# Down projection in four blocks instead of three, with its operands fetched piece by piece ahead of time

## The chip, the cores and the metric

The kernel runs on one NeuronCore of a Trainium2 chip. Its engines are TensorE (PE, with its weight loads shown apart as PEld), VectorE (DVE), ScalarE (ACT), GpSimd (POOL) and SyncE (SP), which here only issues DMAs. The metric is device time in microseconds (us) for one execution, the median of several.

## The reference

One layer of a decoder for 1024 prompt tokens with 16 meta tokens ahead of them, and for 8 running sequences of 4 tokens each. A short convolution and a multi-head retention mix the tokens, `w_out` projects the result back, and a SwiGLU network follows. Only this last part matters here:

```
xn = _rmsnorm(x, norm2_g)
x  = x + (silu(xn @ w_gate) * (xn @ w_up)) @ w_down      # 1024 -> 2816 -> 1024
y  = _rmsnorm(x, final_norm_g)
```

## The kernel before

All activations stand transposed: features on the 128 partitions, the 1056 tokens along the free dimension, cut into two halves `g` of 528 columns (`HT`). Every fp32 operand is split into a high and a low part; a product is three matmuls (high by high, high by low, low by high).

**Gate and up.** The hidden width of 2816 is 22 tiles of 128 (`f`). For each `f` the function `strassen` computes gate and up together by a Winograd scheme with seven products instead of eight. Their right-hand operands (`comb`) are 7 combinations of 8 tiles each; these 56 tiles stand in the pool `rows`, which has 62 buffers of one shape. The results of two neighbouring `f` make a "pair"; `spill` and `spill_plain` write 7 combinations of a pair, or the plain tiles of the last four `f`, to DRAM (`hd`, `hp`), high and low parts apart, 264 KB each, through POOL's queue (`to_hd`, whose two parts take `rows` buffers too).

**Down.** `w_down` is applied in `DBLOCKS`, three blocks of 3 pairs each, and then in a plain part for the last four `f`. A block fetches its 42 operand tiles (7 keys x 3 pairs x 2 parts) from `hd` into `rows` buffers with `pull` (L886 to L889), all ahead of its first matmul in the program's order. Then four iterations over two rows of output tiles (`m`) follow. Each loads four pieces of `w_down` (`load_w`, five buffers `wraw`) and runs `strassen`.

In `strassen`, `product` splits one weight (ACT writes `whi` at L153, DVE writes `wlo` at L155, four buffers each) and then issues its matmuls (L762): pairs x 2 token sets x 3, so 18 for three pairs. Four of the weights are sums that `total` makes on DVE (L750), in buffers `s` of the current pool. The order is `y1 z1 y2 w1 y3 z2 y4` over three accumulators in PSUM (`dy`, `dz`, `dw` in the rows). After each product `on` adds the accumulator to a running sum `x1[m][g]` in SBUF (L913, 128 x 528). So `y2` can write `dy` only when the addition after `y1` has read it.

The 16 tiles `x1` start from the residual, which lies in DRAM as `x1d`. They are allocated in the pool `fin`, which is opened where the pool `late` (gate and up results, the sums of that part) is closed; `fin` takes over its memory. Their loads (L907) stand behind the loads of `w_down` in each iteration of the first block.

The framework orders the instructions of each engine and queue itself when the program is built: an instruction can be placed once its buffer is available, and among those the program's order decides. SP issues its DMAs one after the other, so one that waits for a buffer holds up all behind it.

Of the kernel before, what the change touches and what calls it, by code (L numbers as in the profile page):

```python
# [10 lines left out]
F32 = mybir.dt.float32  # L11
F32R = mybir.dt.float32r
# [4 lines left out]
P = 128  # L17
# [14 lines left out]
KT = DM // P  # L32
NFF = 22
# [12 lines left out]
HT = 528  # L46
# [1 line left out]
PO = [240, 512]  # L48
NDP = 9
NPL = NFF - 2 * NDP  # L50
DBLOCKS = [(0, 3), (3, 6), (6, 9)]

C_CONV_B, C_CONV_C, C_CONV_H, C_Q, C_K, C_V, C_G = 0, 4, 8, 12, 16, 20, 24

# [58 lines left out]
def _build(nc, t, offs, ncols):  # L113
    with tile.TileContext(nc) as tc:
        _body(nc, tc, t, offs, ncols)


def _body(nc, tc, t, offs, ncols):
    PSUM = bass.MemoryType.PSUM
    V, S, G, T, D = nc.vector, nc.scalar, nc.gpsimd, nc.tensor, nc.sync  # L120
    HW = SW // 2
    with contextlib.ExitStack() as ctx:
# [7 lines left out]
        def ut(name, dt=F32):  # L130
            return rows.tile([P, SW], dt, tag="u", name=name)
# [14 lines left out]
        def load_w(ap, n):  # L146
            raw = wts.tile([P, 512], F32, tag="wraw", name="wraw", bufs=5)
            D.dma_start(raw[:, :n], ap)
            return raw
# [48 lines left out]
        def rms_compact(sets, name):  # L198
            blocks = [(i, o, min(P, w - o)) for i, (_, w) in enumerate(sets) for o in range(0, w, P)]
            tot = len(blocks)  # L200
            ps = aux.tile([P, 512], F32, tag="aux", name=name + "p")
            a = cst.tile([P, 16], F32, tag="rms", name=name + "a", bufs=6)
            V.memset(a, 1.0)
            for q in range(len(sets[0][0])):
                for i, (c, o, n) in enumerate(blocks):
                    T.matmul(ps[:n, q * tot + i:q * tot + i + 1], sets[c][0][q][:, o:o + n], ones[:, 0:1],
                             start=True, stop=True)
                i = 0
                while i < tot:
                    j, n = i, blocks[i][2]  # L210
                    while j < tot and blocks[j][2] == n:
                        j += 1
                    if q == 0:
                        V.tensor_scalar(a[:n, i:j], ps[:n, i:j], 1.0 / DM, EPS, ALU.mult, ALU.add)
                    else:
                        V.scalar_tensor_tensor(a[:n, i:j], ps[:n, q * tot + i:q * tot + j], 1.0 / DM, a[:n, i:j],
                                               ALU.mult, ALU.add)
                    i = j
            r = cst.tile([P, 16], F32, tag="rms", name=name + "r", bufs=6)
            tmp = cst.tile([P, 16], F32, tag="rms", name=name + "t", bufs=6)  # L220
            rsqrt(r[:, :tot], a[:, :tot], tmp[:, :tot])
            return r, blocks
# [17 lines left out]
        with contextlib.ExitStack() as mid_ctx:  # L240
# [46 lines left out]
            for k in range(KT):  # L287
# [5 lines left out]
                for s in range(SETS):  # L293
                    if k == 0 and s == 0:
                        h = SW // 2
# [21 lines left out]
            for k in range(KT):  # L317
                for s in range(SETS):
                    n = WALL[s]
# [25 lines left out]
            for s in range(SETS):  # L345
                n = WALL[s]
# [309 lines left out]
        def gg(name):  # L656
            return late.tile([P, SW], F32, tag="gg", name=name, bufs=9)

        def tt(name):
            return late.tile([P, HW], F32, tag="tt", name=name, bufs=4)  # L660
# [5 lines left out]
        for f in range(4):  # L666
            w = w_in(C_G + f)
            for s in range(SETS):
                n = WTOK[s]
                ps = proj(w, xn[s], ntok[s], "pg")  # L670
                x = gg("gt")
# [5 lines left out]
        x1d = dram.tile([KT, 2, P, HT], F32, name="x1d")  # L677
        hd = dram.tile([NDP, 7, 2, P, HT], F32, name="hd")
        hp = dram.tile([NPL, 2, 2, P, HT], F32, name="hp")
# [12 lines left out]
        def norm2(s):  # L692
            n = ntok[s]
            st = [([sums2[s]], WTOK[s])]
            r, bl = rms_compact(st, f"n2{s}")
            yield
            rms_rows(r, bl, st, f"n2{s}",
                     [[(rstd2[g][:, SO[s]:SO[s] + n], g * n, n) for g in range(2)]])
            yield

        for s in range(SETS):
            n = ntok[s]
            ss2 = late.tile([P, SW], F32, tag="rr", name="ss2", bufs=2)
            half = None
            for m in range(KT):
                x = gg("x1")
# [11 lines left out]
                if m % 2 == 0:  # L718
                    c = {"b11": build(s, xg[:, :n], "b11")}
                    t1 = tt("t1")  # L720
# [3 lines left out]
                else:  # L724
                    c["b21"] = build(s, xg[:, :n], "b21")
                    t2, t3, t4 = tt("t2"), tt("t3"), tt("t4")
# [97 lines left out]
        def up_rhs(s, k, key, part):  # L824
            return comb[s][k][key][:, part, :ntok[s]]

        pending = iter(())
        n2g = norm2(1)
        held = None
        for f in range(NFF):  # L830
            wg, wu = t["w_gate"][f], t["w_up"][f]
            a11 = load_w(wg[:, :512], 512)
            a21 = load_w(wu[:, :512], 512)
            a22 = load_w(wu[:, 512:], 512)
            a12 = load_w(wg[:, 512:], 512)
            gt = [gg("gt") for _ in range(2)]
            up = [gg("up") for _ in range(2)]

            def on(step, ps):
                if step == "y1":  # L840
                    S.activation(gt[0][:, :HT], ps, AF.Copy)
                elif step == "z1":
                    S.activation(up[1][:, :HT], ps, AF.Copy)
                elif step == "y2":
                    S.activation(up[0][:, :HT], ps, AF.Copy)
                elif step == "w1":
                    V.tensor_tensor(gt[0][:, :HT], ps, gt[0][:, :HT], ALU.add)
                elif step == "y3":
                    V.tensor_tensor(up[1][:, :HT], ps, up[1][:, :HT], ALU.add)  # L849
                elif step == "z2":  # L850
                    V.tensor_tensor(up[0][:, :HT], ps, up[0][:, :HT], ALU.add)
                else:
                    V.tensor_tensor(gt[1][:, :HT], ps, rstd2[1], ALU.mult)
                if step == "w1":
                    V.tensor_tensor(gt[0][:, :HT], gt[0][:, :HT], rstd2[0], ALU.mult)
                if f == 0 and step in ("y1", "z1"):
                    next(n2g)
                next(pending, None)

            strassen(late, a11, a21, a22, a12, 512, 4, up_rhs, "b", on)  # L860
            for g in range(2):
                x, y = gt[g][:, :HT], up[g][:, :HT]
                S.activation(x, x, AF.Silu)
                V.tensor_tensor(y, y, rstd2[g], ALU.mult)
                V.scalar_tensor_tensor(y, y, -1.0, x, ALU.mult, ALU.mult)
            for _ in pending:
                pass
            if f >= 2 * NDP:
                pending = spill_plain(f - 2 * NDP, *up)
            elif f % 2 == 0:  # L870
                held = up
            else:
                pending = spill(f // 2, *held, *up)
# [4 lines left out]
        fin = ctx.enter_context(tc.tile_pool(name="fin", bufs=1))  # L878
# [1 line left out]
        def tf(name):  # L880
            return fin.tile([P, HW], F32, tag="tt", name=name, bufs=5)

        KEYS = ("b11", "t3", "t2", "b21", "t1", "t4", "b22")
        x1 = [[fin.tile([P, HT], F32, name=f"x1_{m}_{g}") for g in range(2)] for m in range(KT)]

        def pull(src, name):  # L886
            x = ut(name, F32R)
            D.dma_start(x.bitcast(F32)[:, :HT], src)
            return x  # L889

        for bi, (p0, p1) in enumerate(DBLOCKS):
            nk = p1 - p0
            hs = {key: [[pull(hd[p, i, part], "h" + key) for part in range(2)] for p in range(p0, p1)]
                  for i, key in enumerate(KEYS)}

            def dn_rhs(s, k, key, part):
                return hs[key][k][part][:, SO[s]:SO[s] + ntok[s]]

            for m in range(0, KT, 2):
                w = nk * P  # L900
                at = 2 * p0 * P
                a11, a21 = (load_w(t["w_down"][m + i][:, at:at + w], w) for i in range(2))
                a22, a12 = (load_w(t["w_down"][m + i][:, at + w:at + 2 * w], w) for i in (1, 0))
                if bi == 0:
                    for i in range(2):
                        for g in range(2):
                            D.dma_start(x1[m + i][g], x1d[m + i, g])  # L907

                def on(step, ps):
                    i, g = {"y1": (0, 0), "z1": (1, 1), "y2": (1, 0), "w1": (0, 0), "y3": (1, 1), "z2": (1, 0),  # L910
                            "y4": (0, 1)}[step]
                    x = x1[m + i][g]
                    V.tensor_tensor(x, x, ps, ALU.subtract if i else ALU.add)  # L913

                strassen(fin, a11, a21, a22, a12, w, nk, dn_rhs, "d", on)

        hs = [[[pull(hp[i, g, part], "hp") for part in range(2)] for g in range(2)] for i in range(NPL)]
        wd = []
        for m in range(KT):
            raw = load_w(t["w_down"][m][:, 2 * NDP * P:], 512)  # L920
# [20 lines left out]
        for s in range(SETS):  # L941
            for g in range(2):
                n = ntok[s]
                ss3 = tf("ss3")
                for m in range(KT):
# [9 lines left out]
                    x = x1[m][g][:, SO[s]:SO[s] + n]  # L955
# [14 lines left out]
def _host(inp):  # L970
# [13 lines left out]
    for name in ("w_gate", "w_up"):  # L984
        w = f[name][0].reshape(KT, P, NFF * P)[order].reshape(DM, NFF * P)
        a[name] = tiles(w, NFF)
    order = [2 * p + i for p0, p1 in DBLOCKS for i in range(2) for p in range(p0, p1)] + list(range(2 * NDP, NFF))
    a["w_down"] = tiles(f["w_down"][0].reshape(NFF, P, DM)[order].reshape(NFF * P, DM), KT)
# [41 lines left out]
```

## Time and profile before

| what | value |
|---|---|
| median of 3 runs | 1240.03 us (1238.91 to 1240.71) |
| the profiled execution | 1237.07 us |
| its span from the first to the last instruction | 1235.2 us |
[...]
| TensorE busy | 1197.7 us, 97% |
| VectorE busy | 824.0 us, 67% |

The span is what the trace covers; the profiled execution's time is 1.9 us longer. Times in the rows below count from the span's start. The last gate and up step (`f` = 21) runs until 961.8 us, the down blocks from there to 1167.9 us, the plain part and the final norm to the end.

### The profile page before, as it was taken

What the parts mean: (1) busy time and instruction counts of PE and PEld (TensorE: products, weight loads), DVE (VectorE), ACT (ScalarE), POOL (GpSimd) and SP (SyncE); (2) the same over time, 40 slices, a digit from 0 to 9 for tenths busy, and PEclk for the clock granted to TensorE, in tenths of its full rate; (3) what the DMA queues carried; (4) which work ended last, traced back from release to release, by engine and by line L of the source; (5) the groups of instructions that cost most, each with busy time, mean ns of one, the idle gap of its engine ahead of it and who ended that gap; (6) DMA issues with size and microseconds to landing.
All of it is one profiled execution on the core that took longest, in us unless ns stands there. A gap on an engine that the chain in (4) does not pass through costs nothing.

```text
span 1235.2 us, 24336 instructions
## 1 busy us (share of the span) xinstructions
PE 1197.7 (97%) x9769; PEld 1185.0 (96%) x9769; DVE 824.0 (67%) x1520; ACT 480.8 (39%) x904; POOL 121.8 (10%) x251
## 2 busy tenths in 40 slices
PE   8999999999999999999999999999999499999996
PEld 8999988999999999999999999999999499999996
DVE  5355477676454678777977797778775365757665
ACT  8256521121133456534444444444443122212353
POOL 0100121000000112102220222022210000000000
PEclk9999999999999999999999999999999799999998
DMA  6321211101111456324442544255434997666213
GB/s 235 98 70 44 77 44 44 35 18 40 34 53 44 123 172 197 122 74 170 169 144 94 174 166 142 95 175 174 140 125 144 397 303 270 220 239 196 75 40 102
DMA packets 79760, 163.01 MB, mean 132 GB/s; under 512 B 10445, under 2 KB 21472, under 8 KB 79648
## 3 DMA queue, kind: packets, MB, share of 16 engines
q1 hardware_dynamic: 65264, 114.57, 28.6%
q0 software_dynamic: 14384, 46.89, 10.6%
q8 instruction: 77, 1.26, 0.4%
q14 instruction: 35, 0.29, 0.1%
HBM read 113.15 MB, written 48.26 MB: 131 GB/s over the span
## 4 chain that ended last, share of the span: by engine, by line
PE 86%; issue 5%; DMA 4%; DVE 3%; ACT 1%; POOL 1%; SPq 0%; DVEq 0%; POOLq 0%; ACTq 0%
PE by L762 18%; PE bz L762 9%; PE dy L762 9%; PE po L180 6%; PE bw L762 5%; PE dz L762 4%; PE pk L180 4%; PE pc L180 4%; PE pv L180 4%; PE pq L180 4%; PE pg L180 4%; PE pd L951 3%; PE pb L180 3%; PE ph L180 3%; PE dw L762 2%
## 5 line engine op out<-in xcount | busy, mean ns | idle before, releaser
L153 ACT ACTIVATE whi<-wraw 128x512 fp32r<-128x512 f32 (+1 forms) x186 | 113.3, 609 | 317.5 <-issue 63.4
L155 DVE TENSOR_TENSOR wlo<-wraw,whi 128x512 fp32r<-128x512 f32 (+1 forms) x186 | 122.4, 659 | 60.2 <-ACT whi L153 60.1
L153 ACT ACTIVATE whi<-s 128x512 fp32r<-128x512 f32 (+1 forms) x136 | 80.4, 592 | 155.2 <-PE by L762 47.5
L762 PE MATMUL by<-t,whi 128*128 128x256 f32 (+1 forms) x704 | 131.9, 287 | 0.0
L762 PE MATMUL bz<-t,whi 128*128 128x256 f32 (+1 forms) x704 | 131.7, 286 | 0.0
L762 PE MATMUL by<-b,whi 128*128 128x256 f32 (+1 forms) x704 | 129.8, 284 | 0.2 <-DVE up L849 0.2
L155 DVE TENSOR_TENSOR wlo<-s,whi 128x512 fp32r<-128x512 f32 (+1 forms) x136 | 86.9, 639 | 42.6 <-ACT whi L153 42.0
L762 PEld LDWEIGHTS by<-t,whi 128*128 128x128 f32 x704 | 110.3, 190 | 0.0
L762 PEld LDWEIGHTS bz<-t,whi 128*128 128x128 f32 x704 | 109.8, 189 | 0.0
L762 PEld LDWEIGHTS by<-b,whi 128*128 128x128 f32 x704 | 109.3, 188 | 0.4 <-DVE up L849 0.4
L762 PE MATMUL by<-t,wlo 128*128 128x256 f32 (+1 forms) x352 | 100.8, 286 | 0.0
L762 PE MATMUL bz<-t,wlo 128*128 128x256 f32 (+1 forms) x352 | 100.5, 285 | 0.0
L762 PE MATMUL by<-b,wlo 128*128 128x256 f32 (+1 forms) x352 | 100.2, 285 | 0.0
L913 DVE TENSOR_TENSOR x<-x,dy 128x528 f32<-128x528 f32 x48 | 33.8, 704 | 56.2 <-PE dy L762 44.8
L762 PE MATMUL dy<-ht,whi 128*128 128x272 f32 (+1 forms) x288 | 55.7, 291 | 13.7 <-DVE x L913 13.1
L762 PEld LDWEIGHTS by<-t,wlo 128*128 128x128 f32 x352 | 67.0, 190 | 0.0
L762 PEld LDWEIGHTS bz<-t,wlo 128*128 128x128 f32 x352 | 66.6, 189 | 0.0
L762 PEld LDWEIGHTS by<-b,wlo 128*128 128x128 f32 x352 | 66.1, 188 | 0.0
L762 PE MATMUL bw<-b,whi 128*128 128x272 f32 (+1 forms) x352 | 65.5, 285 | 0.0
L788 POOL DMA_DIRECT2D hd<-hh x63 | 34.0, 540 | 284.4 <-ACT hh L786 282.7
L762 PEld LDWEIGHTS dy<-ht,whi 128*128 128x128 f32 x288 | 46.0, 194 | 14.3 <-DVE x L913 13.4
L762 PE MATMUL dz<-ht,whi 128*128 128x272 f32 (+1 forms) x288 | 55.3, 290 | 3.4 <-ACT whi L153 3.4
(303 smaller groups left out, 3194.2 us busy)
## 6 DMA issues: line engine op xcount, KB each, us to landing
ht<-hd SPq DMA_DIRECT2D x72, 264.0 KB, 5.3
hd<-hh POOLq DMA_DIRECT2D x63, 264.0 KB, 3.7
hd<-hl POOLq DMA_DIRECT2D x63, 264.0 KB, 3.7
hb<-hd SPq DMA_DIRECT2D x54, 264.0 KB, 5.3
wraw<-w_in SPq DMA_DIRECT2D x54, 256.0 KB, 2.9
wraw<-w_gate SPq DMA_DIRECT2D x44, 256.0 KB, 2.9
wraw<-w_up SPq DMA_DIRECT2D x44, 256.0 KB, 2.8
wraw<-w_down SPq DMA_DIRECT2D x48, 192.0 KB, 3.5
```

What stands on the lines that cost most here:

```text
L153: S.activation(hi[:, :n], raw[:, :n], AF.Copy)
L155: V.tensor_tensor(lo[:, :n], raw[:, :n], hi.bitcast(F32)[:, :n], ALU.subtract)
L180: T.matmul(ps[:, g, :n], wt[:, sl], xk[part][:, g * n:(g + 1) * n], start=(first and i == 0), stop=(last and i == 2))
L762: T.matmul(out, wt[:, sl], rhs(s, k, key, part), start=(first and k == 0 and i == 0), stop=(k == kt - 1 and i == 2), skip_group_check=not ...
L788: G.dma_start(dst[0], hi.bitcast(F32)[:, :HT])
L913: V.tensor_tensor(x, x, ps, ALU.subtract if i else ALU.add)
L951: T.matmul(ps[:, 0, :n], wt[:, sl], hs[k][g][part][:, SO[s]:SO[s] + n], start=(k == 0 and i == 0), stop=(k == NPL - 1 and i == 2))
```

## The change

The 9 pairs are cut into blocks of 2, 2, 2 and 3 pairs. A block's operand fetches become a generator (`pull_block`, `pull_plain`) that is advanced a few tiles at a time from inside other work: 4 tiles after each of the 7 products of the last gate and up step for block 0 (28 tiles), 1 tile after each of the 28 products of a block for the next block of 2 pairs, 2 tiles per product for the block of 3 pairs, and 1 per product for the 16 tiles of the plain part. What is left is fetched where the block begins. The four first running sums `x1[0..1][0..1]` are moved from `fin` to buffers of `rows`, and their loads stand at the start of the last gate and up step; the other twelve stay in `fin` and are allocated where they are loaded.

```diff
-DBLOCKS = [(0, 3), (3, 6), (6, 9)]
+DBLOCKS = [(0, 2), (2, 4), (4, 6), (6, 9)]
...
+        def pull(src, name, dt=F32R):
+            x = ut(name, dt)
+            D.dma_start(x.bitcast(F32)[:, :HT], src)
+            return x
+
+        def pull_block(b):
+            p0, p1 = DBLOCKS[b]
+            hs = parts[b] = {}
+            for i, key in enumerate(KEYS):
+                hs[key] = []
+                for p in range(p0, p1):
+                    hs[key].append([])
+                    for part in range(2):
+                        hs[key][-1].append(pull(hd[p, i, part], "h" + key))
+                        yield
...
+        def advance(gen, n):
+            for _ in range(n):
+                next(gen, None)
...
         for f in range(NFF):
...
+            if f == NFF - 1:
+                for i in range(2):
+                    for g in range(2):
+                        x1[i][g] = pull(x1d[i, g], "x1", F32)[:, :HT]
+                ahead = pull_block(0)
...
                 next(pending, None)
+                advance(ahead, 4)
...
-        x1 = [[fin.tile([P, HT], F32, name=f"x1_{m}_{g}") for g in range(2)] for m in range(KT)]
...
         for bi, (p0, p1) in enumerate(DBLOCKS):
             nk = p1 - p0
-            hs = {key: [[pull(hd[p, i, part], "h" + key) for part in range(2)] for p in range(p0, p1)]
-                  for i, key in enumerate(KEYS)}
+            for _ in ahead:
+                pass
+            hs = parts[bi]
+            if bi + 1 < len(DBLOCKS):
+                ahead = pull_block(bi + 1)
+                step_n = (DBLOCKS[bi + 1][1] - DBLOCKS[bi + 1][0] + 1) // 2
+            else:
+                ahead, step_n = pull_plain(), 1
...
-                if bi == 0:
+                if bi == 0 and m > 0:
                     for i in range(2):
                         for g in range(2):
+                            x1[m + i][g] = fin.tile([P, HT], F32, name=f"x1_{m + i}_{g}")
                             D.dma_start(x1[m + i][g], x1d[m + i, g])
...
                     V.tensor_tensor(x, x, ps, ALU.subtract if i else ALU.add)
+                    advance(ahead, step_n)
```

## Rows read from the trace of the kernel before

**Rows 1.** The page's part 1: busy us, share, instructions by engine.

```profile
PE 1197.7 (97%) x9769; PEld 1185.0 (96%) x9769; DVE 824.0 (67%) x1520; ACT 480.8 (39%) x904; POOL 121.8 (10%) x251
```

**Rows 2.** Windows of 10 us: length, busy time by engine, clock, DMA share, GB/s.

```profile
960.00:970.00 10.00, 6.65 (x45) 6.35 (x44) 6.84 (x12) 3.76 (x7) 2.16 (x4) 0.87 1.04 396
970.00:980.00 10.00, 3.66 (x28) 3.46 (x26) 2.42 (x5) 1.09 (x3) 0.00 (x0) 0.84 1.04 402
980.00:990.00 10.00, 3.19 (x14) 3.19 (x15) 3.05 (x5) 0.00 (x0) 0.00 (x0) 0.50 1.05 389
```

**Rows 3.** Waits of PE from 962 to 987 us: total, times, longest.

```profile
PE dy L762 <- DVE x L913: 13.1, 1, 13.1
PE dz L762 <- ACT whi L153: 3.4, 1, 3.4
```

**Rows 4.** Timeline of PE, 961 to 995 us: start, us, instruction, idle before.

```profile
961.77 0.41 PE L762 MATMUL dy<-hb,whi 128*128 128x272 f32 x2
...
967.47 0.82 PE L762 MATMUL dz<-ht,whi 128*128 128x272 f32 x2 [3.35 <-ACT whi L153]
...
971.32 0.42 PE L762 MATMUL dw<-hb,whi 128*128 128x272 f32 x2
...
986.81 0.82 PE L762 MATMUL dy<-ht,whi 128*128 128x272 f32 x2 [13.15 <-DVE x L913]
```

**Rows 5.** Timeline of SP's queue, 925 to 1000 us.

```profile
928.11 20.85 SPq L148 DMA_DIRECT2D wraw<-w_down  x4
949.05 3.56 SPq L888 DMA_DIRECT2D hb<-hd  x6
...
976.60 3.70 SPq L888 DMA_DIRECT2D hb<-hd  x6
980.66 2.30 SPq L907 DMA_DIRECT2D x<-x1d  x4
...
998.75 0.85 SPq L888 DMA_DIRECT2D hb<-hd  x2
```

**Rows 6.** Timelines of DVE and ACT around the block's start.

```profile
966.22 1.03 DVE L750 TENSOR_TENSOR s<-wraw 128x384 f32<-128x384 f32 x2
...
986.05 0.70 DVE L913 TENSOR_TENSOR x<-x,dy 128x528 f32<-128x528 f32 x1 [11.30 <-DMA x<-x1d]
...
966.89 0.52 ACT L153 ACTIVATE whi<-s 128x384 fp32r<-128x384 f32 x1 [1.45 <-DVE s L750]
```

**Rows 7.** Chain that ended last, down blocks: start, us, work.

```profile
1035.01 2.20 PE dw L762 x18
...
1066.44 2.19 PE dw L762 x18
...
1097.05 2.19 PE dw L762 x18
...
1128.68 2.17 PE dw L762 x18
...
1167.92 15.05 PE pd L951 x120
```

**Rows 8.** Groups by form, 990 to 1168 us: busy, mean ns, idle before.

```profile
L913 DVE TENSOR_TENSOR x<-x,dy 128x528 f32<-128x528 f32 x47 | 33.1, 704 | 44.9 <-PE dy L762 44.8
...
L155 DVE TENSOR_TENSOR wlo<-s,whi 128x384 fp32r<-128x384 f32 x44 | 24.3, 552 | 0.9 <-ACT whi L153 0.7
...
L153 ACT ACTIVATE whi<-s 128x384 fp32r<-128x384 f32 x44 | 23.1, 524 | 68.5 <-PE dy L762 43.4 <-PE dz L762 14.5 <-DVE s L750 9.2
```

**Rows 9.** Groups by form, VectorE, 1168 to 1220 us: an operation 256 wide.

```profile
L956 DVE TENSOR_TENSOR x<-pd,x 128x256 f32<-128x256 f32 x14 | 5.8, 421 | 4.3 <-PE pd L951 4.2
```

**Rows 10.** Timeline of DVE, 880 to 905 us: operations close behind each other.

```profile
882.19 0.71 DVE L799 TENSOR_TENSOR dt<-up 128x528 f32<-128x528 f32 x1
882.81 0.70 DVE L803 TENSOR_TENSOR dt<-up 128x528 f32<-128x528 f32 x1
```

**Rows 11.** Timeline of ACT, 1040 to 1062 us: the first weight of block 1.

```profile
1048.78 0.53 ACT L153 ACTIVATE whi<-wraw 128x384 fp32r<-128x384 f32 x1 [6.71 <-DMA wraw<-w_down]
```

More of the change, by code (lines that the diff above doesn't have):

```diff
@@ L825, in up_rhs, with pull_plain @@
             return comb[s][k][key][:, part, :ntok[s]]
+        KEYS = ("b11", "t3", "t2", "b21", "t1", "t4", "b22")
+        def pull(src, name, dt=F32R):
+            x = ut(name, dt)
+            D.dma_start(x.bitcast(F32)[:, :HT], src)
+            return x
+        parts = {}
+        def pull_block(b):
[8 more added lines that the diff above has]
+                        yield
+        def pull_plain():
+            hs = parts["plain"] = []
+            for i in range(NPL):
+                hs.append([])
+                for g in range(2):
+                    hs[-1].append([])
+                    for part in range(2):
+                        hs[-1][-1].append(pull(hp[i, g, part], "hp"))
+                        yield
+        def advance(gen, n):
+            for _ in range(n):
+                next(gen, None)
         pending = iter(())
+        ahead = iter(())
         n2g = norm2(1)
         held = None
+        x1 = [[None] * 2 for _ in range(KT)]
         for f in range(NFF):
@@ L837, in _body @@
             up = [gg("up") for _ in range(2)]
+            if f == NFF - 1:
+                for i in range(2):
+                    for g in range(2):
+                        x1[i][g] = pull(x1d[i, g], "x1", F32)[:, :HT]
+                ahead = pull_block(0)
             def on(step, ps):
@@ L881, in tf @@
             return fin.tile([P, HW], F32, tag="tt", name=name, bufs=5)
-        KEYS = ("b11", "t3", "t2", "b21", "t1", "t4", "b22")
-        x1 = [[fin.tile([P, HT], F32, name=f"x1_{m}_{g}") for g in range(2)] for m in range(KT)]
[L886 to L889, printed above, removed]
         for bi, (p0, p1) in enumerate(DBLOCKS):
             nk = p1 - p0
-            hs = {key: [[pull(hd[p, i, part], "h" + key) for part in range(2)] for p in range(p0, p1)]
-                  for i, key in enumerate(KEYS)}
+            for _ in ahead:
[6 more added lines that the diff above has]
+                ahead, step_n = pull_plain(), 1
             def dn_rhs(s, k, key, part):
@@ L913, in on @@
                     V.tensor_tensor(x, x, ps, ALU.subtract if i else ALU.add)
+                    advance(ahead, step_n)
                 strassen(fin, a11, a21, a22, a12, w, nk, dn_rhs, "d", on)
-        hs = [[[pull(hp[i, g, part], "hp") for part in range(2)] for g in range(2)] for i in range(NPL)]
+        for _ in ahead:
+            pass
+        hs = parts["plain"]
         wd = []
```

## Prediction

> **What bounds the kernel now.** The page's first part says TensorE: 97% busy [rows 1]. The windows of 10 us say where it is not: from 960 to 990 us it is busy for 13.5 us of 30 and its clock falls to half, while the DMA engines move 389 to 402 GB/s and are full [rows 2]. The list of TensorE's waits names two: 13.1 us for an addition of VectorE to a running sum, and 3.4 us for a weight [rows 3]. The timelines tell the story. The down part's first matmul starts at 961.77. After `y1` TensorE stands for 3.35 us: `z1` needs the sum `s3`, which lies in `fin`, so VectorE can write it only when gate and up have let go of that memory, at 966.22 [rows 4, 6]. Then `z1` and `w1` run, and `y2` waits until 986.81, because `dy` is still full: the addition after `y1` starts at 986.05 and had waited 11.3 us for its tile of `x1d` [rows 4, 6]. SP's queue says why that tile was late: the 42 operand fetches went out from 949.05 to 980.66, the first loads of `x1` behind them [rows 5]. So it is not the operands of `y2` that are missing but 264 KB of residual at the end of a full queue.
>
> **What this costs.** One iteration of a block of 3 pairs takes 15.30 us (1066.44 to 1097.05 is two) [rows 7]: 126 matmuls of 0.1214 us. Twelve make 183.6 us; the part takes 961.77 to 1167.92, 206.15 us [rows 4, 7]. [...]
>
> **The change part by part.** The matmuls stay: 9 pairs x 7 products x 6 x 4 iterations = 1512 at 0.1214 us, 183.6 us. A product of 2 pairs has 12 and lasts 1.46 us, an iteration 10.2 us. So the sum is over what is lost.
>
> *First running sums in `rows` buffers.* They no longer wait for `fin`, and no longer stand behind all fetches. This removes the 13.15 us and the restart after it. It leaves the wait for `s3`.
>
> *Term 1, the wait for `s3`.* VectorE's chain at the end of gate and up is unchanged, so `s3` starts at 966.22 as before. The addition after `y1`, ready from 963.3, I put into a pause of that chain at no cost; it would cost 0.7 us if it went ahead of the chain. `s3` is now 256 wide: 0.42 us by a VectorE operation of that width [rows 9]; its split on ScalarE 0.42 (0.52 at 384 wide [rows 8], two thirds of it at least, 0.35). With the two hand-overs of 0.12 and 0.06 us that stand between these steps before [rows 4, 6], `z1` starts at 967.2. `y1` is shorter and ends at 963.2. The wait grows from 3.35 to 4.0 us. It would be 2.5 if `w1`, whose weight needs no sum, were placed ahead of `z1`. I take 4.0.
>
> *Term 2, the restart at the lower clock*: 1.7 us as before [rows 4]; 0 to 2.5 (the larger restart above).
>
> *Term 3, block changes*: three instead of two, 0.93 us each as the mean of the two [rows 7]: 2.8 us. Before, the first weight of block 1 came late: ScalarE waited 6.7 us for its piece of `w_down` [rows 11], queued behind fetches that waited for buffers. Now 62 buffers less 4 for `x1` hold 56 tiles of two neighbouring 2-pair blocks, so there only the change to the 3-pair block (28 + 42 = 70 tiles) must wait for buffers. Bounds: 0.8 (that one alone) and 4.
>
> *Term 4, the second pair of `x1` rows.* `x1[2..3]` still lie in `fin` and are behind other fetches. SP's pace in the full stretch is 31.6 us for 42, 0.75 us each, and a tile was usable 5.4 us after its issue (980.66 to 986.05) [rows 5, 6]. What bars the queue until 949.05 are `w_down` loads waiting for `wraw` [rows 5]; they stand later in the program than the fetches and yet ahead in the queue, so I assume the same start. 28 fetches then end at 970.1 and have landed at 975.5; `y4`, the last to need them, starts at 967.2 + 5 products of 1.46 + 1.7 = 976.2. That just holds. Behind them stand 7 fetches for block 1 (5.3 us) and four half-sized weight loads (1.4): `x1[2]` goes out at 976.8, is there at 982.2, and its addition is done at 982.9. The second iteration's `y1` ends at 979.1 and `z1` at 980.6, so `y2` waits 2.3 us. If the queue starts once the first `comb` buffers come free, around 944, it is 0; if the four first sums also go out after 949 it is 5.3.
>
> *Smaller operations on VectorE and ScalarE.* 84 products of 2 pairs now carry one split, one addition and 4/7 of a sum each. On VectorE the addition stays 0.70 us [rows 8], split and sum are 0.42 [rows 9] instead of 0.55 [rows 8]. Operations close behind each other start 0.62 us apart though each shows 0.70 [rows 10], so I take 0.08 off each: 0.62 + 0.34 + 0.19 = 1.15 us per product of 1.46, and 1.30 where a sum falls. Before it had 1.44 of 2.19. The cover shrinks from 0.7 to 0.3 us, but it is there: cost 0. If nothing overlapped, the products with a sum would need 0.70 + 0.42 + 0.42 = 1.54 us, 0.08 too much, 48 times: 3.9 us. ScalarE has 0.42 of 1.46: nothing.
>
> [...]
>
> *The rest.* The plain part's 16 tiles fit beside 42 + 4 in the 62 buffers; its weight splits need 16 more, which come free six per product in the last iteration of 15.3 us: 0, at most 2. In the last gate and up step the four sums take buffers that the spills use: 0, at most 1, hidden since SP and POOL run ahead of that step.
>
> **Sum.** 4.0 + 1.7 + 2.8 + 2.3 = 10.8 us lost instead of 22.5: 11.7 us gained. The profiled execution took 1237.07 us (span 1235.2), so 1225.4; the median of the runs shown is 3 us above it, so 1228.
>
> **The rivals.**
>
> *The wait moves to the next `x1` rows (slower).* While `fin` is still closed, SP's queue may be filled with all 28 fetches of block 1, whose buffers are already free, ahead of `x1[2]`. For it: the queue took loads out of the program's order already [rows 5]. Against it: before, once `fin` was open, the `x1` loads went ahead of the next block's fetches, which begin at 998.75 [rows 5]. Price: 21 more fetches at 0.75 is 15.8 us, so a wait of 18.1 and one more restart of 1.7: lost 4.0 + 1.7 + 2.8 + 18.1 + 1.7 = 28.3, 5.8 us more than before: 1246 us. It makes the kernel slower than before from some 13 fetches beyond the 7. With 3 to 6 beyond, the time is 1232 to 1234.
>
> *The restart is filled.* `w1` goes ahead of `z1` (wait 2.5 us, clock kept) and the queue starts at 944: lost 2.5 + 2.8 = 5.3, time 1223. For it: `w1`'s operands are now there earlier. Against: `z1` stood first before [rows 4].
>
> *VectorE becomes the bound* in the 2-pair blocks: 1228 + 3.9 = 1232; more if its queue holds an addition behind a split, since `y2` has now 1.46 us instead of 2.19 for the addition after `y1`. Against: VectorE's idle time ahead of those additions is 45 us in 47 [rows 8].
>
> *The change does little*: the fetches go out no earlier, since the `w_down` loads still bar the queue. That is in the forecast already; the gain hangs on `x1` alone. If even `x1[0..1]` stayed behind the fetches, 28 x 0.75 puts it at 970.1 + 5.4 instead of 986.05: still 10 us better, less the shorter cover: 1232.
>
> **How the numbers follow.** Forecast 0.55, range of its own 1224 to 1232 (terms 3 and 4 at their bounds); restart filled 0.15; VectorE 0.08; `x1[2]` partly late 0.10, wholly late 0.07; little done 0.05. A range from 1220 to 1237 leaves out the wholly late case, some of the partly late one and the lowest end of the filled one. About 0.2% (2.5 us) is what a measurement of this kernel can tell from no change. Faster than 1237.5: all but the wholly late case and part of the partly late one, 0.89; within 0.2%: 0.04; slower: 0.07.
>
> **What would show it.** In the profile after: no wait of 13 us of `dy` on an addition; the first addition right after `y1`; a wait of `dz` for `whi` of about 4 us near 963, followed by matmuls at half the clock; `dy` groups of 12 in 1.46 us in the blocks of 2; VectorE's share there near 80%; at the second iteration `x1` loads issued near 977 and a wait of some 2 us. Wrong if TensorE waits for additions throughout the 2-pair blocks, or if a long wait stands in the second iteration, or if the four first sums go out after the operand fetches.

## The result and the profile after

The changed kernel took 1223.12 us (median of 4 runs, 1221.23 to 1224.78), the kernel before 1239.47 (4 runs, 1237.61 to 1240.71): ratio 0.9869, 95% interval 0.9848 to 0.9890, so 14 to 19 us faster. The forecast was 1228. The profiled execution took 1221.23 us, its span is 1219.5 us. In some executions the down part starts 965.2 to 966.8 us after the span's start instead of 960.1 to 961.9, with a granted clock of 0.91 from 40 to 60 us and 0.83 from 180 to 200 instead of 1.00 (last section), so kernels are compared below by the length of the down part as well.

Part 1 of the page shows the same matmuls [rows 1] in 3.0 us less of busy time, and VectorE with 72 instructions more:

```profile
PE 1194.7 (98%) x9769; PEld 1182.5 (97%) x9769; DVE 845.1 (69%) x1592; ACT 486.3 (40%) x932; POOL 121.8 (10%) x251
```

TensorE's waits from 880 to 1235 us (total, times, longest; those of the final norm left out). The 13.1 us for an addition [rows 3] are gone; the wait of `dz` is left and one of 1.7 us is new:

```profile
PE dz L762 <- ACT whi L153: 3.6, 1, 3.6
PE dy L762 <- ACT whi L153: 1.7, 1, 1.7
```

The first two windows of [rows 2] (length, busy time by engine, clock, DMA share, GB/s), and one of 100 us from 980:

```profile
960.00:970.00 10.00, 6.41 (x43) 6.17 (x42) 7.65 (x15) 3.26 (x7) 2.14 (x4) 0.86 1.05 400
970.00:980.00 10.00, 8.28 (x65) 8.11 (x65) 6.74 (x15) 2.45 (x6) 0.00 (x0) 0.97 1.03 371
...
980.00:1080.00 100.00, 100.00 (x826) 100.00 (x825) 85.29 (x178) 27.93 (x69) 0.00 (x0) 1.00 0.85 287
```

From 980 on TensorE is never idle, through two block changes, beside a VectorE that is 85% busy. So all that the down part still loses lies in its first 18 us. The timeline of PE there:

```profile
961.93 0.42 PE L762 MATMUL dy<-hb,whi 128*128 128x272 f32 x2
...
967.15 0.74 PE L762 MATMUL dz<-ht,whi 128*128 128x272 f32 x2 [3.59 <-ACT whi L153]
...
971.75 0.42 PE L762 MATMUL dw<-hb,whi 128*128 128x272 f32 x2
...
977.98 0.48 PE L762 MATMUL dy<-hb,whi 128*128 128x272 f32 x2 [1.72 <-ACT whi L153]
```

`z1` and `y2` together take 4.60 us instead of 2.92: the clock had fallen (the granted clock is 0.52 from 967.15 to 969.96, while `z1` runs). The wait at 977.98 is that of `y4`. Its row names a split on ScalarE, but the split that ended last before it belongs to the second iteration; `y4`'s own was done by 973. What was missing is in the timeline of DVE:

```profile
976.39 0.87 DVE L750 TENSOR_TENSOR s<-wraw 128x256 f32<-128x256 f32 x2 [1.96 <-DMA wraw<-w_down]
977.18 0.70 DVE L954 TENSOR_TENSOR x<-x,dy 128x528 f32<-128x528 f32 x1
```

The addition after `y3`, which frees `dy` for `y4`, stands in VectorE's queue behind two weight sums for the second iteration, and these wait for `w_down`. It ends at 977.88, and `y4` starts 0.10 us later. SP's queue shows where that piece was:

```profile
928.27 6.23 SPq L148 DMA_DIRECT2D wraw<-w_down  x2
941.99 1.80 SPq L831 DMA_DIRECT2D hb<-hd  x4
...
960.93 2.04 SPq L831 DMA_DIRECT2D hb<-hd  x4
...
964.06 2.29 SPq L831 DMA_DIRECT2D hb<-hd  x4
966.72 1.70 SPq L831 DMA_DIRECT2D ht<-hd  x3
968.52 2.56 SPq L148 DMA_DIRECT2D wraw<-w_down  x3
972.33 3.30 SPq L948 DMA_DIRECT2D x<-x1d  x4
```

Block 0's fetches start at 941.99, not 949.05 [rows 5]; before, four `w_down` loads stood ahead of them, here two. They end at 962.97. Seven fetches for block 1 follow, ahead of the `w_down` loads of 968.52. The chain that ended last, with the `dw` groups of [rows 7] (some left out):

```profile
968.52 7.85 DMA wraw<-w_down
...
984.03 1.45 PE dw L762 x12
...
1004.39 1.45 PE dw L762 x12
...
1014.56 1.46 PE dw L762 x12
...
1086.03 1.46 PE dw L762 x12
...
1098.42 2.18 PE dw L762 x18
...
1144.22 2.18 PE dw L762 x18
```

The load takes 7.85 us to land. From 984.03 to 1086.03 are ten iterations, 10.20 us each. The one across the first block change (1004.39 to 1014.56) takes 10.17, and the stretch across the last one (1086.03 to 1098.42) takes 12.39, which is four products of 1.46 and three of 2.18: block changes cost nothing now.

**The balance.** From the first `dy` matmul to the first of the plain part, the down part takes 961.93 to 1152.79, 190.9 us; before it was 961.77 to 1167.76, 206.0 (the chain of [rows 7] gives that end 0.16 later). So 15.1 of the 15.8 us between the two profiled executions lie here, and 0.7 in what follows (66.7 us to the span's end against 67.4). The work alone is 12 x 10.20 + 4 x 15.27 (three iterations from 1098.42 to 1144.22 are 45.80) = 183.5 us, so 7.4 us are lost: 3.8 before `z1`, 1.7 by the lower clock, 1.9 before `y4`.

### The profile page after: what moved, and what is told of

It reads as the page before. It is cut to its first block, busy times and chain, and to the rows that moved or that the text cites. A ratio compares the mean times of both kernels' runs of the same rounds, so it can differ in the third digit from the quotient of the medians.

```text
span 1219.5 us, 24549 instructions
## 1 busy us (share of the span) xinstructions
PE 1194.7 (98%) x9769; PEld 1182.5 (97%) x9769; DVE 845.1 (69%) x1592; ACT 486.3 (40%) x932; POOL 121.8 (10%) x251
## 4 chain that ended last, share of the span: by engine, by line
PE 87%; issue 5%; DVE 4%; DMA 3%; POOL 1%; ACT 1%; SPq 0%; DVEq 0%; POOLq 0%; ACTq 0%
PE by L762 19%; PE bz L762 9%; PE dy L762 8%; PE po L180 6%; PE bw L762 5%; PE dz L762 4%; PE pk L180 4%; PE pc L180 4%; PE pd L995 4%; PE pv L180 4%; PE pq L180 4%; PE pg L180 4%; PE pb L180 3%; PE ph L180 3%; PE dw L762 2%
## 5 line engine op out<-in xcount | busy, mean ns | idle before, releaser
L153 ACT ACTIVATE whi<-wraw 128x512 fp32r<-128x512 f32 (+2 forms) x198 | 115.6, 584 | 291.7 <-issue 62.9
L155 DVE TENSOR_TENSOR wlo<-wraw,whi 128x512 fp32r<-128x512 f32 (+2 forms) x198 | 124.2, 628 | 58.7 <-ACT whi L153 58.6
L153 ACT ACTIVATE whi<-s 128x512 fp32r<-128x512 f32 (+2 forms) x152 | 83.6, 551 | 162.3 <-PE by L762 48.5
L155 DVE TENSOR_TENSOR wlo<-s,whi 128x512 fp32r<-128x512 f32 (+2 forms) x152 | 89.3, 588 | 40.5 <-ACT whi L153 40.3
L954 DVE TENSOR_TENSOR x<-x,dy 128x528 f32<-128x528 f32 x64 | 45.0, 703 | 25.6 <-PE dy L762 24.6
L762 PE MATMUL dz<-ht,whi 128*128 128x256 f32 (+1 forms) x288 | 55.0, 288 | 3.6 <-ACT whi L153 3.6
L762 PE MATMUL dy<-hb,whi 128*128 128x256 f32 (+1 forms) x288 | 53.3, 284 | 1.7 <-ACT whi L153 1.7
L762 PEld LDWEIGHTS bw<-b,whi 128*128 128x128 f32 x352 | 54.5, 188 | 0.0
```

What stands on the lines that cost most here:

```text
L153: S.activation(hi[:, :n], raw[:, :n], AF.Copy)
L155: V.tensor_tensor(lo[:, :n], raw[:, :n], hi.bitcast(F32)[:, :n], ALU.subtract)
L762: T.matmul(out, wt[:, sl], rhs(s, k, key, part), start=(first and k == 0 and i == 0), stop=(k == kt - 1 and i == 2), skip_group_check=not ...
```

## The experiments

Each ratio is against the kernel before as it ran beside that experiment (its medians there are 1237.29 to 1239.47). Beside the ratio the table has the length of the down part, from the first `dy` matmul to the first of the plain part, in the profiled execution. It comes from one execution of each kernel, so a difference of a us or two in it is not safe. "Sums" are the first four `x1` tiles in `rows`, "blocks" 2, 2, 2, 3 pairs, "ahead 0" block 0's fetch inside the last gate and up step, "ahead between" the later blocks' fetches inside the block before.

| label | what | median us | ratio, 95% interval | down part us |
|---|---|---|---|---|
| (before) | nothing | 1239.47 | 1 | 206.0 |
| (changed) | sums, blocks, ahead 0, ahead between | 1223.12 | 0.9869 (0.9848 to 0.9890) | 190.9 |
| e1_sums_only | sums | 1232.75 | 0.9966 (0.9946 to 0.9986) | 200.3 |
| e2_blocks_only | blocks | 1232.77 | 0.9957 (0.9941 to 0.9973) | 200.3 |
| e9_sums_and_blocks | sums, blocks | 1232.99 | 0.9961 (0.9947 to 0.9974) | 200.5 |
| e10_ahead_between | all but ahead 0 | 1227.69 | 0.9909 (0.9888 to 0.9931) | 195.4 |
| e11_ahead_first | all but ahead between | 1223.25 | 0.9872 (0.9850 to 0.9895) | 190.1 |
| e4_sums_in_fin | all but sums | 1224.99 | 0.9890 (0.9865 to 0.9916) | 193.6 |
| e3_three_blocks | all but blocks | 1239.11 | 1.0007 (0.9994 to 1.0020) | 206.8 |
| e12_ahead_first_late | e11 with later fetches | 1224.16 | 0.9889 (0.9868 to 0.9911) | 193.1 |
| e6_packed_weights | changed, `w_down` in two loads | 1221.48 | 0.9862 (0.9833 to 0.9891) | 190.0 |
| e5_sums_in_late | changed, weight sums in `late` | 1222.44 | 0.9883 (0.9855 to 0.9911) | 192.5 |
| e7_both | e5 and e6 | 1222.35 | 0.9874 (0.9850 to 0.9899) | 188.9 |
| e8_one_pair | changed, blocks of 2, 1, 1, 2, 3 | 1243.10 | 1.0040 (1.0023 to 1.0057) | 211.7 |

### One part alone

The kernel before with only the sums moved, only the blocks cut, or both; fetches at each block's head.

```diff
-        x1 = [[fin.tile([P, HT], F32, name=f"x1_{m}_{g}") for g in range(2)] for m in range(KT)]
+            if f == NFF - 1:                       # e1 and e9
+                for i in range(2):
+                    for g in range(2):
+                        x = ut("x1")
+                        D.dma_start(x[:, :HT], x1d[i, g])
+                        x1[i][g] = x[:, :HT]
...
-DBLOCKS = [(0, 3), (3, 6), (6, 9)]
+DBLOCKS = [(0, 2), (2, 4), (4, 6), (6, 9)]         # e2 and e9
```

> The kernel before (blocks of 3 pairs, a block's 42 fetches ahead of it) with one part of the change: the four first running sums in rows buffers, loaded at the start of the last gate and up step. My theory (the late 264 KB of residual was the stall): the 13.1 us wait of dy on an addition and the restart after it are gone; the wait for s3 (3.4), its restart (1.7) and the two block changes (1.8) stay; with 42 fetches at 0.75 us from about 944 to 949 on the last operands of block 0 land between 980 and 986, so y3, z2 and y4 wait 1 to 5 us: 1226 to 1231. Rival (the operands' fetch sets the start of the down part, so that early sums alone gain little): 1235 or more. Rival (the sums are the whole change): 1223.

> The kernel before with the block sizes alone changed to 2, 2, 2, 3 pairs; all x1 in fin, behind the block's fetches. My theory: x1 now stands behind 28 fetches instead of 42, so its first addition starts 10 us earlier, near 976; lost about 4 + 1.7 at z1, 4.5 + 1.7 at y2, and little at the block changes: 1228 to 1233, with dy still waiting for an addition. Rival (the fetch must be spread over other work, sizes alone do nothing): 1239. Rival (VectorE can't carry the smaller products): slower than 1240.

> Two parts of the change, early first sums and blocks of 2, 2, 2, 3; a block's fetches stand at the head of that block in the program as before, not inside other work. My theory (the queue's order comes from which buffers are free, so the place of the fetches in the program matters little): within 2 us of the changed kernel, 1222 to 1226, and no loss at the changes between blocks of 2, since 56 tiles and 4 sums fit in 62 buffers. Rival (fetching inside the other block's work empties the block changes): 1 us lost at each of three changes, 1226 to 1228.

e2 came out as expected; e1 took 1232.75 us (1226 to 1231 expected) and e9 1232.99 (1222 to 1226 expected). Each part gives 5 to 6 us of the down part, and both together give no more than one alone. The sums do remove the wait of 13.1 us, and smaller blocks shorten it to 5.3 us; but in e9 TensorE stands again at the first block change, now for a weight. There, the timelines of ACT and then PE:

```profile
1021.15 0.42 ACT L153 ACTIVATE whi<-wraw 128x256 fp32r<-128x256 f32 x1 [11.46 <-DMA wraw<-w_down]
```

```profile
1021.62 0.82 PE L762 MATMUL dy<-hb,whi 128*128 128x272 f32 x2 [6.49 <-ACT whi L153]
```

and SP's queue in e9:

```profile
932.52 20.85 SPq L148 DMA_DIRECT2D wraw<-w_down  x4
953.46 2.65 SPq L897 DMA_DIRECT2D hb<-hd  x4
...
979.21 7.75 SPq L148 DMA_DIRECT2D wraw<-w_down  x3
...
995.37 0.85 SPq L897 DMA_DIRECT2D hb<-hd  x2
...
1016.03 3.04 SPq L148 DMA_DIRECT2D wraw<-w_down  x5
```

Four `w_down` loads that wait for buffers bar the queue until 953.46, three more from 979.21 to 986.96. Block 1's first weight goes out at 1016.03, behind its 28 fetches, 49.9 us after the down part's start (966.18), and is late. In e2 the same weight goes out at 1016.38, and TensorE waits 1.8 us for it: what e9 saves before that point it waits at that point, 6.5 us. So it is not true that the gain hangs on `x1` alone.

### Which of the two fetches ahead

```diff
-                ahead = pull_block(0)          # e10: not in the last gate and up step
-                advance(ahead, 4)
+        ahead = pull_block(0)                  # e10: at the block's head
...
-            for _ in ahead:
+            for _ in ahead if bi == 0 else pull_block(bi):     # e11: later blocks at their heads
-                    advance(ahead, step_n)
```

> The changed kernel with block 0's 28 fetches back at the head of the down part; between blocks the fetches stay inside the other block's work. Lengths are from the first dy matmul to the first pd matmul; before 206.0 us, changed 190.9, with early sums and small blocks alone 200.5. New theory (what the early sums gave back was lost at the first block change, because block 1's fetches stood behind all x1 and weight loads of block 0): the 6.5 us wait at the first block change and its restart go, 191 to 194 us, 1223 to 1227. Rival (the gain of fetching ahead is the earlier start of block 0's fetch, 942 instead of 953): 198 us or more, 1231.

> The changed kernel with only block 0 fetched ahead, inside the last gate and up step; every later block is fetched at its own head as before. New theory: a wait of 5 to 8 us and a restart at the change to block 1 come back, 197 to 201 us for the down part. Rival (the earlier start of block 0 carries the gain): 191 to 193 us.

e10 lies between its theory (191 to 194) and its rival (198 or more); e11 went the rival's way (191 to 193). Without the early fetch of block 0 the down part is 195.4 us, without the others it is 190.1, no longer than in the changed kernel. e11 differs from e9 in where block 0 is fetched (and in that the other `x1` tiles are allocated where they are loaded), and is 10.4 us shorter; how much of that is the second difference, no run shows. With all else as in the changed kernel the early fetch is worth 4.6 us (e10, 195.42 against 190.86). The queue of e11:

```profile
945.48 1.79 SPq L831 DMA_DIRECT2D hb<-hd  x4
...
982.98 0.85 SPq L831 DMA_DIRECT2D hb<-hd  x2
...
1005.81 3.03 SPq L148 DMA_DIRECT2D wraw<-w_down  x5
```

Block 1's fetches still stand ahead of its first weights, as in e9, but these go out 40.4 us after the down part's start (965.42) instead of 49.9, and TensorE doesn't wait. The queue gains on e9 twice: the first fetch is 7.2 us earlier against that start (19.9 ahead of it instead of 12.7), and loads of `w_down` go out singly and no longer bar the queue for 7.75 us. The window of 20 us before the down part's start (length, PE busy, clock, DMA share, GB/s), first e9, then e11:

```profile
946.18:966.18 20.00, 20.00 (x166) 1.00 0.76 261
```

```profile
945.42:965.42 20.00, 20.00 (x166) 1.00 0.97 356
```

In e11 the DMA engines move 95 GB/s more in the 20 us ahead of the part, 1.9 MB or 7 fetches, while TensorE is busy all the same. In e10 the rate there is 258 GB/s. e10 is still 5 us better than e9: block 1's 28 fetches are spread between the loads of block 0, and its first weight goes out at 1004.27, 41.6 us after the down part's start (962.71) instead of 49.9. Its loss is earlier: the second iteration's `z1` waits 2.0 us for a sum of late `w_down`.

### The fetch ahead without the small blocks, and without the sums

```diff
-DBLOCKS = [(0, 2), (2, 4), (4, 6), (6, 9)]
+DBLOCKS = [(0, 3), (3, 6), (6, 9)]                      # e3
...
-                        x1[i][g] = pull(x1d[i, g], "x1", F32)[:, :HT]
-                if bi == 0 and m > 0:
+                if bi == 0:                             # e4: all x1 in fin
```

> The changed kernel with three blocks of 3 pairs; early sums and fetching ahead stay. New theory: 42 + 42 + 4 tiles don't fit in 62 buffers, so 26 of the next block's fetches wait for buffers until the last iteration and the weights of the next block's first iteration queue behind them: 1 to 4 us lost at each of two changes, 193 to 198 us. Rival (fetching ahead alone empties the changes, whatever the block size): 190 to 192 us, the same as the changed kernel.

> The changed kernel with all sixteen x1 tiles back in fin, loaded in the first block. My theory: the x1 loads wait for fin and stand behind the 28 fetches of block 0, so dy waits for its first addition until about 975: 4 + 1.7 at z1, 3 to 5 + 1.7 at y2: 1226 to 1231. Rival (the early fetch of operands carries the gain): within 1 us of the changed kernel, 1223.

With blocks of 3 nothing is gained (206.8 us; theory and rival had 193 to 198 and 190 to 192), and e1, with the same blocks and sums but no fetch ahead, is better with 200.3. The second iteration's `z1` shows it (DVE, PE, then SP's queue):

```profile
989.61 1.14 DVE L750 TENSOR_TENSOR s<-wraw 128x384 f32<-128x384 f32 x2 [7.67 <-DMA wraw<-w_down]
```

```profile
990.86 0.82 PE L762 MATMUL dz<-ht,whi 128*128 128x272 f32 x2 [7.48 <-ACT whi L153]
```

```profile
969.63 8.94 SPq L831 DMA_DIRECT2D hb<-hd  x12
...
984.36 1.70 SPq L148 DMA_DIRECT2D wraw<-w_down  x3
```

Fetches for block 1 went ahead of the loads of `w_down` which the running block needed; that is the changed kernel's wait of 1.7 us in large. Here 14 fetches of block 1 stand ahead, in the changed kernel seven. Without the moved sums (e4) the kernel keeps most of the gain, between what theory (1226 to 1231) and rival (1223) had foretold: block 0's fetch starts at 932.98 there, and the first `x1` loads go out at 963.88 instead of 980.66 [rows 5]. So by these executions the sums are worth 2.7 us in this company, 5.7 by themselves.

### Does the start carry it, or the order?

```diff
-                advance(ahead, 4)
+                if step in ("y3", "z2", "y4"):
+                    advance(ahead, 10)
```

> The kernel in which only block 0 is fetched ahead, but its fetches go out during the last three products of the last gate and up step instead of during all seven, so that one more load of w_down stands ahead of them in the queue. Theory (what carries the gain is that the first block's fetch starts before the queue is barred by loads of w_down that wait for their buffers): the fetch starts 2 to 5 us later than the 945.5 of the kernel with only block 0 ahead, and the down part grows from 190.1 towards 195 us, near 1228. Rival (what carries it is the order behind, weights ahead of the next block's fetches, not the start): the down part stays at 189 to 191.5 us, 1223.

SP's queue and one row of DVE in e12:

```profile
926.97 15.63 SPq L148 DMA_DIRECT2D wraw<-w_down  x3
942.69 1.88 SPq L831 DMA_DIRECT2D hb<-hd  x4
```

```profile
972.30 0.42 DVE L750 TENSOR_TENSOR s<-wraw 128x256 f32<-128x256 f32 x1 [3.49 <-DMA wraw<-w_down]
```

Starts must be counted from the down part's start, which is 960.63 in e12 and 965.42 in e11, for the clock reason given with the result. So counted, three `w_down` loads instead of two stand ahead of the fetches, and these start 17.9 us ahead of the part instead of 19.9. Three of the second iteration's four `w_down` loads go out 5.0, 6.1 and 8.25 us after the part's start in both kernels, so the order behind is the same. The down part is 3.0 us longer, which is the theory's way and not the rival's (189 to 191.5). It is lost where VectorE waits 3.49 us for a weight sum of the second iteration, with additions of the first behind it and TensorE idle for 2.17 us (0.8 in e11). This speaks for the start, but on one execution each; the medians, 1224.16 and 1223.25, don't differ by more than the runs spread.

### What is left: the wait before `z1` and the late weight

```diff
-                x = pool.tile([P, 512], F32, tag="ws", name=nm, bufs=4 if n > 384 else 2)
+                x = pool.tile([P, 512], F32, tag="ws", name=nm, bufs=4 if n > 384 or pool is late else 2)
...
+        fin = late                    # e5, e7: late is closed, fin opened, after the first iteration
...
+                if nk == 2:           # e6, e7: both pieces of a row of w_down in one load
+                    r0, r1 = (load_w(t["w_down"][m + i][:, at:at + 2 * w], 2 * w) for i in range(2))
+                    a11, a12, a21, a22 = r0[:, :w], r0[:, w:], r1[:, :w], r1[:, w:]
```

> The changed kernel with the two pieces of w_down that lie side by side loaded by one DMA in the blocks of 2 pairs: two loads of 256 KB for each iteration instead of four of 128 KB, in the same five buffers, so 2.5 iterations fit instead of 1.25. In the changed kernel TensorE stood for 1.7 us before y4 of the first iteration; the addition that it needed stood behind a weight sum on VectorE that waited for a w_down piece issued at 968.5. Theory (that late piece is the cause): the wait goes, 189 us, 1.9 us less than the changed kernel. Rival (the x1 loads of the second iteration, or the fetch of b22, are late as well): 190.5 to 191 us, with a wait at the same place.

> The changed kernel with the first iteration's weight sums in the buffers of gate and up, so that the second weight sum needn't wait for the new memory. Theory (the wait before z1 and its restart, 3.6 + 1.7 us, are plain lost time): TensorE's wait for dz near 963 is gone, the time is about 1218 us and the down part about 185.5 us. Rival (the next thing is late right behind it: the second iteration's weight pieces, which landed at 976.4 behind the operand fetches): the time saved comes back as a wait of 4 to 6 us before the last product of the first iteration or the first of the second, and the time is 1221 to 1223 us.

> The edit of the weight sums together with w_down in two packed loads an iteration in the blocks of 2 pairs instead of four. Theory (two separate losses): the wait before z1 and the one behind the late piece of w_down are both gone, the time is about 1217 us, the down part 184.5 to 186 us. Rival (operand fetches are next to be late, since 28 of them take 21 us from 942): a wait for an operand or a weight of 2 us or more appears between 960 and 980, the time is 1220 us or more.

Packed loads remove the 1.7 us wait, as their theory had it, but the down part gets only 0.8 us shorter (190.03 against 190.86): `z1` and `y2` take 5.43 us there instead of 4.60, the clock staying low for longer (`y2` alone takes 2.62 us there, 1.79 in the changed kernel; the granted clock is 0.69 from 960 to 970 us, against 0.86). The sums in `late` remove the wait and the restart at `z1`, and the part gets 1.6 us longer in this execution: waits of 0.7 and 1.9 us for weights follow, since ScalarE waits 2.19 and 4.38 us for `w_down`, then three waits of 0.9 us for the low part of a weight, and stretches of slow clock (0.88 granted from 970 to 980 us, 0.95 from 980 to 990). With both, the longest wait is 1.5 us, for an addition whose `x1` had not landed, and the part is 188.9 us. None is faster than the changed kernel by more than its runs spread; the times of 1217 and 1218 that the theories of e7 and e5 gave didn't come, those of their rivals did. The windows of e7 speak for the DMA engines as the next bound:

```profile
965.19:985.19 20.00, 17.97 (x144) 1.00 1.05 398
985.19:1005.19 20.00, 19.18 (x153) 1.00 1.05 393
```

For 40 us the DMA engines are full (share 1.05) and move 393 to 398 GB/s. By that, a wait removed there only brings TensorE sooner to the next tile in the queue. This is argued, not shown: a version with less to move in these 40 us wasn't tried.

### Where VectorE becomes the bound

```diff
-DBLOCKS = [(0, 2), (2, 4), (4, 6), (6, 9)]
+DBLOCKS = [(0, 2), (2, 3), (3, 4), (4, 6), (6, 9)]
```

> The changed kernel in blocks of 2, 1, 1, 2 and 3 pairs. A product of one pair is 0.73 us of matmuls. Theory (VectorE's operations overlap as taken in the prediction: 0.62 for the addition, 0.21 for a split and 0.12 for 4/7 of a sum, 128 columns wide, 0.95 us): VectorE bounds the 56 products of one pair, 0.22 us each, and the time is 12 us longer than the changed kernel, near 1235 us. Rival 1 (they do not overlap, 1.16 us a product): 24 us longer, near 1247. Rival 2 (VectorE's work is hidden at any size, or the clock alone matters): within 3 us of the changed kernel.

The down part grew by 20.8 us, 0.37 us for each of the 56 products of one pair, which so take 1.10 us instead of 0.73. (Five steady iterations of such blocks, 1024.07 to 1063.23, give 1.12.) That lies between the two sizes foretold. The timeline of DVE in such a block:

```profile
1043.14 0.70 DVE L954 TENSOR_TENSOR x<-x,dz 128x528 f32<-128x528 f32 x1 [0.51 <-PE dz L762]
1043.76 0.28 DVE L155 TENSOR_TENSOR wlo<-s,whi 128x128 fp32r<-128x128 f32 x1
1043.96 0.28 DVE L155 TENSOR_TENSOR wlo<-wraw,whi 128x128 fp32r<-128x128 f32 x1
```

and TensorE's waits from 1010 to 1090 us:

```profile
PE dz L762 <- DVE wlo L155: 5.3, 6, 0.9
PE dy L762 <- DVE x L954: 4.2, 7, 0.6
```

Operations start 0.20 us (128 wide) and 0.62 us (528 wide) apart, 0.08 less than each lasts, as the theory took; the remaining 0.15 us per product is VectorE idle in its turn (the 0.51 us at 1043.14), since the two engines now wait for each other. So a quarter of the columns costs 0.20 of 0.62 us of queue, a third.

## Why the prediction was right, and where not

**Right: the removed wait, term 1 and term 2.** No wait of 13 us is left. `z1` was to start at 967.2 and did at 967.15; its wait was to be 4.0 us, by the starts it is 3.8. The restart was to cost 1.7 and did: before, `z1` took 3.85 us instead of 2.19 (granted clock 0.57 from 967.47 to 971.32). The 2.5 at the top of its range is what was left over of the 22.5 us lost before (206.15 less 183.6), and no run shows it as such; in the second restart before, `y2` took 4.12 us instead of 2.19 (granted clock 0.50 from 986.81 to 990.93). VectorE was to keep up, with a share near 80% in the 2-pair blocks: it has 85%, which is 1.24 us of 1.46 per product and not 1.15, and TensorE lost nothing to it. e8 shows that this margin was real but not wide. (The 1.44 us per product before is 1.36 when the 0.08 is taken off every operation; nothing hangs on it.)

**Wrong: term 3.** Three block changes were put at 0.93 us each, 2.8 in all; they cost 0. The rows for that price were of blocks whose first weight came behind fetches that waited for buffers [rows 7, 11]. This changed in the new order, which I had seen for the buffers but not for the weight.

**Half right: term 4.** 2.3 us were foretold, 1.9 came. But it is not `x1[2]` in the second iteration: it is a piece of `w_down` behind seven fetches of block 1, in the first iteration, and it reaches TensorE by VectorE's queue. The seven fetches are only part of its cause: in e11, where they come later, the same load goes out 5.0 us after the part's start instead of 6.6, and still TensorE waits 0.8 us. The size agrees by chance: for a queue that starts near 944 the prediction itself had 0 here.

**Wrong: "the gain hangs on `x1` alone" and "I assume the same start".** The fetches start 7 us earlier, since the last step's fetches pass two of the four `w_down` loads that barred the queue. And the moved sums alone give 5.7 of 15.1 us (e1). Without the early fetch the waiting comes back at the first block change (e9), for which the prediction had 0.93 us. The early fetch of block 0 comes to 10.4 us beside the other two parts (e9 against e11, with the place where `x1` is allocated in it) and to 4.6 in the changed kernel (e10); the fetches between blocks add nothing to it (e11). With blocks of 3 and both kinds of fetches ahead nothing is left of the gain (e3); blocks of 3 with the early fetch alone were not run. That the earlier start works by itself, and not only by the order of `w_down` loads that comes with it, e12 makes likely and does not prove.

**The numbers.** For the profiled execution 1225.4 was foretold, 1221.2 came: 2.8 by term 3, 0.4 by term 4, 0.2 by term 1, 0.7 in the final part. The median was taken 3 us above that execution and is 1.9 above. The rival "the restart is filled" has the right time, 1223, and the right start of the queue (944; 942 was measured), but `z1` still stood first and the restart was not filled. That the clock is kept through a wait of 2.5 us, as it assumed, no run shows: after the wait of 1.72 us the granted clock was 1.00 (977.98 to 979.44), but after one of 2.17 us in e12 the next product took 2.78 us instead of 1.46. "Wholly late `x1[2]`" fell: these loads went out at 972.33, behind seven fetches, not 28. The same crowding with larger blocks did make the gain vanish (e3), with weights late in place of `x1`.

## What to carry to other kernels

SP's queue issued in order, and a load that waited for its buffer cost what stood behind it (in e9 four such loads took the queue for 20.85 us ahead of block 0's fetches, and three more for 7.75 us). In such a queue look for the transfer that starts late while the DMA engines have room (261 GB/s in the 20 us before the stage in e9, 393 to 400 at a share of 1.05) and put its issue ahead of the barring one. Parts of such a change don't add up: two gave 5.7 us each and 5.5 together, three gave 15.9 (e11), so a gain read off one wait must be checked against the next late thing in the same queue. Fetches ahead for the next block cost time where they passed the loads that the running block needed: with blocks of 3, all the fetching ahead made 200.3 us into 206.8.

## What the runs showed of the hardware

The clock's fall didn't come at a fixed place behind a wait. After 3.59 us `z1` ran slow from its start in the changed kernel (12 matmuls in 2.81 us, granted clock 0.52 from 967.15 to 969.96). In e12, after 3.61 us, only its first three matmuls were slow (0.68 us from 965.86; the other nine took 1.14, 0.127 each), and `y2`, 1.8 us later, was slow from start to end (12 in 2.64 us from 967.68, against 1.46 at a granted clock of 1.00). And some executions lose clock where the profile shows TensorE busy all the time: the windows 40 to 60 and 180 to 200 us in the changed kernel and then in e11 (length, PE busy, clock, DMA share, GB/s), a part of the program that is the same in both:

```profile
40.00:60.00 20.00, 20.00 (x165) 1.00 0.39 121
180.00:200.00 20.00, 19.98 (x145) 1.00 0.24 80
```

```profile
40.00:60.00 20.00, 20.00 (x154) 0.91 0.32 102
180.00:200.00 20.00, 20.00 (x115) 0.83 0.19 67
```

11 and 30 matmuls fewer were done, and the down part of e11 starts at 965.42 instead of 961.93. The profiles of e2, e7 and e9 show both falls as well (0.91 and 0.83, the down part from 965.19 to 966.76), that of e10 the second alone (0.83, from 962.71); e1, e3 and e4 show neither (1.00 in both windows). Why only some executions show it stays open.
